# Feed-forward gate and up as pairs of seven half-depth products, hidden rows through DRAM, the down projection as its own stage

## The chip, the cores and the metric

One core of one Trainium2 chip runs the whole program. The metric is device time in microseconds (us) from launch to end, median of several runs. Five engines work side by side, each strictly in the order of its own program: PE (matrix products), DVE (vector), ACT (scalar and lookup functions), POOL (GpSimd) and SP, which here only issues DMAs. Waits between engines are semaphores.

## The reference, cut to what matters

Two blocks run one after the other on a sequence of 1024 tokens of width 1024, in fp32. The change concerns the feed-forward half of the first block:

```python
D_FF = -(-8 * D_MODEL // (3 * 256)) * 256          # 2816 = 22 chunks of 128
xn = rms_norm(x, ffn_norm_g[l])
gate, up = jnp.split(xn @ w_gate_up[l], 2, axis=-1)
x = x + (jax.nn.silu(gate) * up) @ w_down[l]
```

After it the second block (modulation, projections, window attention, convolution, a mixture of 16 experts) follows, and the change leaves its arithmetic as it was.

## The kernel before, in words

Every fp32 operand is held as a high and a low fp32r part, and a product is three matrix instructions: high by high, high by low, low by high (`mm3`, L64 to L67). Raw weights come by DMA into tiles `wst`; ACT copies the high part to `wh` (L58) and DVE subtracts to get `wl` (L59). That pair of instructions is `split`. `Weights.get` hands out the next converted piece and, before that, converts as many pieces ahead as `ahead` says; `fill` issues the next weight DMA on SP when a staging tile is free.

The feed-forward works on chunks of 128 of the 2816 hidden rows, 22 in all, in five parts of 5, 5, 4, 4, 4 chunks. `xn` holds the normed tokens, transposed, as eight tiles of 128 x 1024. For each chunk `columns` (L475) multiplies gate over the full depth of 1024 and two halves of 512 tokens, then up: 2 x 2 x 8 x 3 = 96 matrix instructions of 128x512. DVE scales gate by the token's 1/rms (`rsb`, L1100), ACT takes Silu (L1101), DVE multiplies by up (L1107) and by 1/rms (L1108), and the hidden rows are split to `hH` and `hL` at once. After each part its rows are multiplied with `w_down` in two groups of four output columns (`columns_k`, L279) and added to the resident `x1` (L1124). Between chunks `mods` (L1077) loads one of 48 pieces of the second block's modulation weights and accumulates it with two or four DVE instructions (L1056, L1058).

The second block already has a stage of the kind that the change adds: `quads` multiplies two weight columns as a 2 x 2 block matrix with seven half-depth products in place of eight. `seven` makes the weight combinations on POOL (L153, L154, L158, L162), `quarters` makes those of the tokens. The order on each engine is the order in which the Python code calls it; there is no scheduler.

Of the kernel before, what the change touches and what calls it, by code (L numbers as in the profile page):

```python
# [18 lines left out]
P = 128  # L19
# [3 lines left out]
def fused(tc, x, mix_norm_g, w_in, b_f, sgu_ln_g, sgu_ln_b, w_s, b_s, out_norm_g, w_out,  # L23
# [45 lines left out]
    class Weights:  # L69


        def __init__(self, es, units, side=R, stage=3, hl=3, ahead=2, scols=2112, pcols=1056, name="w"):
# [12 lines left out]
            self.wait, self.spare, self.halves, self.tmp = [], [], False, None  # L85
# [35 lines left out]
        def fill(self):  # L121
            while self.ndma < self.lim:
# [11 lines left out]
                if axis == "s":  # L134
                    self.wait.append(t)
                    if len(self.wait) == 2:
                        self.todo.extend(self.seven(*self.wait))
                        self.wait = []
                else:
                    for i in range(n):  # L140
                        s = t[:, i * cut:(i + 1) * cut, :] if axis == "k" else t[:, :, i * cut:(i + 1) * cut]
                        self.todo.append((lambda s=s, pre=pre: ([f(s) for f in pre], s)[1], int(i == n - 1)))
                self.ndma += 1

        def seven(self, a, b):
# [15 lines left out]
            def make4():  # L161
# [117 lines left out]
    def columns_k(W, n, rH, rL, ks, evac, cut=None, mid=()):  # L279
# [654 lines left out]
    npre = len(units) + 5 * len(pairs)  # L934
# [140 lines left out]
    xh = lambda k, hf: xn[k][0][:, hf * 512:(hf + 1) * 512]  # L1075
    xhl = lambda k, hf: xn[k][1][:, hf * 512:(hf + 1) * 512]
# [8 lines left out]
    def fw_done():  # L1085
        nonlocal psg, pmo
        es_fw.close()
        psg = pool(es_sg, "psg", 2)
        pmo = pool(es_mo, "pmo", 2)

    psg = pmo = None
    for f0, n in parts:
        hT = []
        for f in range(f0, f0 + n):
            sg = [None, None]

            def ev_gate(hf, ps):
                cs = slice(hf * 512, hf * 512 + 512)
                sg[hf] = psg.tile([P, 512], F32, name="sg")
                DVE.tensor_tensor(sg[hf], rsb[:, cs], ps, op=OP.mult)  # L1100
                act(sg[hf], sg[hf], AF.Silu)  # L1101

            hH, hL = phh.tile([P, T], F32R, name="hH"), phh.tile([P, T], F32R, name="hL")

            def ev_up(hf, ps):
                cs = slice(hf * 512, hf * 512 + 512)
                DVE.tensor_tensor(sg[hf], sg[hf], ps, op=OP.mult)  # L1107
                DVE.tensor_tensor(sg[hf], sg[hf], rsb[:, cs], op=OP.mult)  # L1108
                split(hH[:, cs], hL[:, cs], sg[hf])

            if f:
                columns(W, xh, xhl, KD, ev_gate)
                mods()
                columns(W, xh, xhl, KD, ev_up)
            else:
                columns_k(W, 2, xh, xhl, range(KD), lambda c, hf, ps: (ev_gate, ev_up)[c](hf, ps),
                          mid={(FM[0], 1): ffn_rs, (FM[1], 1): lambda: (spread(rsb, rs1), fw_done()), (FM[2], 1): lambda: W.prime(1)})
            hT.append((hH, hL))
            mods()
# [12 lines left out]
    es_s1.close()
# [72 lines left out]
    d_y = dram.tile([KD, P, T], F32, name="d_y")  # L1205
    d_gc = dram.tile([KD, P, T], F32, name="d_gc")
# [50 lines left out]
    rs1b = pool(es_x1, "prs1", 1, R).tile([P, T], F32, name="rs1b")  # L1257

# [22 lines left out]
    W.halves = True  # L1281
# [872 lines left out]
```

## Time and profile before

| | us |
|---|---|
| median of 3 runs | 2988.65 (2987.81 to 2989.24) |
| profiled execution, its own time | 2987.78 |
| its span, first to last instruction | 2985.8 |
| feed-forward of the first block, first to last product | 485.5 to about 1225 |
| seven-product stage of the second block | about 1378 to 1765 |
| PE busy over the span | 2859.5 (96%) |

The profile gives each engine's busy time. A matrix instruction of 128x512 is shown with 0.39 us, but one starts every 0.227 us since they are pipelined; a steady PE is read from the starts, not from the durations. DVE and ACT instructions overlap a little too: in a run without waits a DVE instruction of 128x512 starts 0.60 us after the one before it, although it is shown with 0.68 or 0.69 us.

### The profile page before, as it was taken

How to read it: one execution, taken by the hardware profiler on the slowest of the kernel's cores; microseconds unless marked ns; L12 is line 12 of the kernel's file. 1: busy time of each engine (PE TensorE's matmuls, PEld its weight loads, DVE VectorE, ACT ScalarE, POOL GpSimd, SP SyncE). 2: the span in 40 equal slices, each digit the busy share in tenths (PEclk: the TensorE clock that was granted, in tenths of full speed). 3: DMA queues.
4: the chain of work that ended last, by engine and by line, in shares of the span. 5: the costliest groups of instructions: out<-in, count | busy, mean ns of one | idle time of the engine just before them, and what ended most of it. 6: DMA issues, size and time to landing. Idle time of an engine off the chain costs nothing.

```text
span 2985.8 us, 37222 instructions
## 1 busy us (share of the span) xinstructions
PE 2859.5 (96%) x13943; PEld 2389.1 (80%) x13943; DVE 1911.1 (64%) x2741; ACT 1362.7 (46%) x2127; POOL 596.9 (20%) x607
## 2 busy tenths in 40 slices
PE   8999999999999999999999989899899789999997
PEld 7887878888888888887888877777788678888885
DVE  4446854645354444876666643888732579999998
ACT  5346943211111212522223331788622468888886
POOL 2301322000000000334444411233121302111113
PEclk9999999999999999999999999999999889999998
DMA  5120140322222221242222264000343689999998
GB/s 201 36 78 22 42 150 29 105 79 95 67 99 85 99 74 61 94 146 78 85 85 85 91 227 162 15 15 15 124 150 137 229 309 373 371 378 377 376 376 289
DMA packets 295236, 441.27 MB, mean 148 GB/s; under 512 B 14300, under 2 KB 143040, under 8 KB 294928
## 3 DMA queue, kind: packets, MB, share of 16 engines
q1 hardware_dynamic: 278048, 379.73, 36.8%
q0 software_dynamic: 15520, 58.11, 5.7%
q8 instruction: 109, 1.79, 0.2%
q10 hardware_dynamic: 1488, 1.06, 0.1%
q14 instruction: 71, 0.58, 0.1%
HBM read 380.62 MB, written 58.23 MB: 147 GB/s over the span
## 4 chain that ended last, share of the span: by engine, by line
PE 81%; DVE 7%; ACT 4%; issue 4%; DMA 3%; POOL 1%; SPq 0%; POOLq 0%; DVEq 0%; ACTq 0%
PE b L67 24%; PE b L65 24%; PE b L66 24%; PE pt L1614 1%; DVE pl L1632 1%; PE b L1995 1%; DVE sm L1595 1%; PE po L1644 1%; DVE wl L59 1%; DVE qs L1499 1%; PE pt L777 1%; DMA y<-d_y 1%; DMA d_x<-b,idxT 1%; PE po L1645 1%; PE b L1837 0%
## 5 line engine op out<-in xcount | busy, mean ns | idle before, releaser
L59 DVE TENSOR_TENSOR wl<-wst,wh 128x1024 fp32r<-128x1024 f32 (+3 forms) x620 | 714.3, 1181 | 256.6 <-ACT wh L58 248.9
L58 ACT ACTIVATE wh<-wst 128x1024 fp32r<-128x1024 f32 (+3 forms) x620 | 594.9, 976 | 458.1 <-PE b L66 190.8
L65 PE MATMUL b<-xn,wh 128*128 128x512 f32 x1040 | 408.1, 392 | 6.8 <-ACT xn L58 5.8
L67 PE MATMUL b<-xn,wl 128*128 128x512 f32 x1040 | 406.9, 391 | 3.7 <-DVE wl L59 3.7
L66 PE MATMUL b<-xn,wh 128*128 128x512 f32 x1040 | 406.8, 391 | 0.5 <-DVE xn L59 0.5
L65 PE MATMUL b<-wh,a 128*128 128x512 f32 x768 | 302.4, 394 | 0.2 <-ACT a L58 0.2
L66 PE MATMUL b<-wl,a 128*128 128x512 f32 x768 | 299.9, 391 | 0.8 <-DVE wl L59 0.8
L67 PE MATMUL b<-wh,a 128*128 128x512 f32 x768 | 299.8, 390 | 0.4 <-DVE a L59 0.4
L65 PEld LDWEIGHTS b<-xn,wh 128*128 128x128 f32 x1040 | 196.4, 189 | 47.9 <-ACT xn L58 6.2
L67 PEld LDWEIGHTS b<-xn,wl 128*128 128x128 f32 x1040 | 196.3, 189 | 46.4 <-DVE wl L59 5.2
L66 PEld LDWEIGHTS b<-xn,wh 128*128 128x128 f32 x1040 | 196.2, 189 | 41.7 <-DVE xn L59 1.0
L67 PEld LDWEIGHTS b<-wh,a 128*128 128x128 f32 x768 | 144.5, 188 | 31.1 <-DVE a L59 1.1
L66 PEld LDWEIGHTS b<-wl,a 128*128 128x128 f32 x768 | 144.7, 188 | 30.6 <-DVE wl L59 1.6
L65 PEld LDWEIGHTS b<-wh,a 128*128 128x128 f32 x768 | 144.8, 188 | 29.7 <-ACT a L58 0.7
L2037 POOL DMA_INDIRECT d_x<-b,idxT x15 | 65.8, 4388 | 470.9 <-DVE b L2031 470.9
L241 POOL TENSOR_SCALAR small<-small 128x1 f32<-128x1 f32 (+3 forms) x15 | 5.7, 383 | 768.7 <-ACT xn L1156 680.2
L65 PE MATMUL b<-hH,wh 128*128 128x512 f32 x352 | 137.7, 391 | 0.0
L67 PE MATMUL b<-hH,wl 128*128 128x512 f32 x352 | 137.1, 389 | 0.0
L66 PE MATMUL b<-hL,wh 128*128 128x512 f32 x352 | 136.9, 389 | 0.0
L58 ACT ACTIVATE hH<-sg 128x512 fp32r<-128x512 f32 x44 | 27.8, 632 | 202.7 <-DVE sg L1108 202.7
L1101 ACT ACTIVATE sg<-sg 128x512 f32<-128x512 f32 x44 | 27.7, 632 | 179.7 <-DVE sg L1100 179.7
L1595 DVE CUSTOM_DVE_ANT_0 sm<-sp,mk,nsk 128x640 f32<-128x640 f32 (+1 forms) x128 | 107.0, 837 | 1.2 <-PE sp L1584 1.0
(567 smaller groups left out, 6297.5 us busy)
## 6 DMA issues: line engine op xcount, KB each, us to landing
wst<-in_w_exp_gate_dram SPq DMA_DIRECT2D x128, 512.0 KB, 11.7
wst<-in_w_exp_up_dram SPq DMA_DIRECT2D x128, 512.0 KB, 10.7
wst<-in_w_exp_down_dram SPq DMA_DIRECT2D x128, 512.0 KB, 11.2
wst<-in_w_in_dram SPq DMA_DIRECT2D x74, 512.0 KB, 4.7
mw<-in_w_mod_dram SPq DMA_DIRECT2D x48, 512.0 KB
wst<-in_w_gate_up_dram SPq DMA_DIRECT2D x44, 512.0 KB, 4.0
wst<-in_w_down_dram SPq DMA_DIRECT2D x16, 512.0 KB, 3.8
wst<-in_w_out_dram SPq DMA_DIRECT2D x10, 512.0 KB, 4.7
```

The lines of the kernel that those rows point to most:

```text
L58: act(h, src, AF.Copy)
L59: DVE.tensor_tensor(l, src, rd(h), op=OP.subtract)
L65: PE.matmul(ps, lh, rh, start=start, stop=False)
L66: PE.matmul(ps, lh, rl, start=False, stop=False)
L67: PE.matmul(ps, ll, rh, start=False, stop=stop)
L777: PE.transpose(pt[:, b * P:(b + 1) * P], sm[:, (k0 + b) * P:(k0 + b + 1) * P], ident)
L1499: DVE.tensor_tensor(q[64:128, cs], pt[64 * o:64 * o + 64], rd(q[0:64, cs]), op=OP.subtract)
L1595: DVE.tensor_tensor_reduce(sms[n][:, :nk], sps.pop(n)[:, 256:256 + nk], (mk if i else mk0)[:, :nk], -0.125, nsk[:, hd:hd + 1], op0=OP.add, ...
L1614: PE.transpose(pt[:, hh * P:(hh + 1) * P], sms[4 * u + hh][:, kb * P:(kb + 1) * P], ident)
L1632: DVE.tensor_tensor(pl, pt, rd(ph), op=OP.subtract)
L1644: PE.matmul(pos[u], v, ph, start=kb == 0, stop=False)
L2037: nc.gpsimd.indirect_dma_start(out=d_x2, out_offset=bass.IndirectOffsetOnAxis(ap=idxT[:, e:e + 1], axis=0), in_=y, in_offset=None, compute ...
```

## The change

The first three chunks run gate and up as before. During chunks 1 and 2 `quarters_x` forms four combinations of the token quarters (`TX`). From chunk 3 on, gate and up of a chunk are one pair of weight columns and go through `quads` with seven products of four depth tiles, 84 matrix instructions. The scaling by 1/rms is now a POOL instruction (`times`), four of them for each pair, between the DVE sum and ACT's Silu. The products gate x up are formed at the start of the next pair (`hidden_out`), and the raw hidden rows go to DRAM by a DMA that POOL issues. `x1` goes to DRAM as well, for the time in which its place holds `TX`. After chunk 21 a stage of its own reads the hidden rows back, splits them (`h_in`), reads `x1` back and does the down projection, with four calls of `mods` after each group of columns. DRAM tiles `d_y` and `d_gc` of the second block become one tile for each index.

```diff
+    NCL = 3
+    for f in range(FF):
+        units += [(wsrc(w_gate_up, 0, KD, c * P, P), *(("s", 0) if f >= NCL else ("c", P))) for c in (f, FF + f)]
...
+    for k in range(KD):
+        nc.gpsimd.dma_start(d_xs[k], x1[k])
...
+    def quarters_x(k):
+        a11, a12, a21, a22 = [halft(n) for n in ("s", "u", "c1", "c2")]
+        for o, i, j in ((a11, 0, 0), (a12, 0, 1), (a22, 1, 1), (a21, 1, 0)):
+            DVE.tensor_tensor(o, *[rd(a[:, k, :]) for a in XQ[i, j]], op=OP.add)
+        for o, x, y in ((a11, a12, a11), (a12, a22, a12), (a22, a22, a11), (a21, a21, a22)):
+            DVE.tensor_tensor(o, x, y, op=OP.subtract)
+        for i, t in ((1, a11), (3, a12), (2, a22), (4, a21)):
+            h, l = TX[i]
+            split(h[:, k, :], l[:, k, :], t)
+
+    def hidden_out(h, c1, c2, su, f):
+        DVE.tensor_tensor(h[:, h1], su["u"], c2, op=OP.mult)
+        DVE.tensor_tensor(h[:, h0], su["s"], c1, op=OP.mult)
+        nc.gpsimd.dma_start(d_h[f], h)
...
+            if f == NCL - 1:
+                W.ahead = 4
...
+            while flush:
+                flush.popleft()()
+            c1, c2 = halft("c1"), halft("c2")
+            def times(x, cs):
+                POOL.tensor_tensor(x, x, rsb[:, cs], op=OP.mult)
+                return x
+            def gate(x, cs):
+                act(x, times(x, cs), AF.Silu)
+            su = {}
+            quads(W, SEVX, halft, lambda s, b: gate(plus(c1, s, b), h0),
+                  lambda u, b: (gate(plus(u, u, b), h1), su.update(u=u)),
+                  lambda s, b: (times(plus(s, s, b), h0), su.update(s=s)), lambda s, b: times(plus(c2, s, b), h1))
+            flush.append(lambda hr_=hr_, c1=c1, c2=c2, su=su, f=f: hidden_out(hr_, c1, c2, su, f))
+            mods()
...
+    for _ in range(2):
+        h_load(next(nxt))
...
+            for _ in range(4):
+                mods()
```

`quads` itself is moved up and takes the weights, the tokens and the tiles as arguments:

```python
after = [lambda: act(s, bk[0], AF.Copy), lambda: q11(s, bk[1]),
         lambda: DVE.tensor_tensor(s, s, bk[2], op=OP.add),
         lambda: DVE.tensor_tensor(u, s, bk[3], op=OP.add),
         lambda: (DVE.tensor_tensor(s, s, bk[4], op=OP.add), q22(s, bk[3])),
         lambda: q12(u, bk[5]), lambda: q21(s, bk[6])]
```

Products are numbered 1 to 7 below, and so are the seven weight halves of a pair. Half 3 and half 4 need L153 and L154 on POOL, half 5 needs L158, half 6 needs L162. With `ahead` at 4, the call of `get` for product i converts half i+4, so halves 1 to 4 of the next pair are converted during products 4 to 7 of this one.

First place, POOL in the feed-forward. Before, it has the sums of squares (`s1`), the two small instructions for 1/rms, and then nothing until two small ones for the context tokens (`small`, 128x2) and the last part's squares (`xn`):

```order
L1005 TENSOR_TENSOR s1_3918<-s1_3918,hH_4574 128x512
L1005 TENSOR_TENSOR s1_3918<-s1_3918,hH_4577 128x512
L241 TENSOR_SCALAR small_71<-small_71 128x8
L242 TENSOR_TENSOR small_71<-small_71,mhalf_66 128x8
L241 TENSOR_SCALAR small_71<-small_71 128x2
L242 TENSOR_TENSOR small_71<-small_71,mhalf_66 128x2
L1174 TENSOR_TENSOR xn_8900<-xn_8900,xn_8972 128x512 x2
```

Now each pair has nine, shown from the scaling of `c2` of one pair to that of `c1` of the next (`s1` holds 1/rms by then, `hr` the finished rows):

```order
L1182 TENSOR_TENSOR c2_5276<-c2_5276,s1_3907 128x512
L153 TENSOR_TENSOR ws1_5373<-wst_5164 128x512
L154 TENSOR_TENSOR ws2_5374<-ws1_5373,wst_5162 128x512
L1182 TENSOR_TENSOR u_5278<-u_5278,s1_3907 128x512
L1182 TENSOR_TENSOR s_5277<-s_5277,s1_3907 128x512
L1139 DMA d_h4_4598<-hr_5271 128x1024
L158 TENSOR_TENSOR wst_5164<-wst_5162,wst_5164 128x512
L162 TENSOR_TENSOR wst_5162<-wst_5162,ws2_5374 128x512
L1182 TENSOR_TENSOR c1_5424<-c1_5424,s1_3907 128x512
```

The combinations for halves 5 and 6 stand behind the DMA of the rows before, and those for halves 3 and 4 behind the scaling of `c2`.

Second place, DVE over the end of a chunk. Before (`sg` gate, then hidden rows; `acc0`, `acc1` the modulation sums):

```order
L59 TENSOR_TENSOR wl_5184<-wst_4893,wh_5183 128x1024
L1100 TENSOR_TENSOR sg_5214<-s1_3918,b_5189 128x512
L1100 TENSOR_TENSOR sg_5242<-s1_3918,b_5217 128x512
L1058 SCALAR_TENSOR_TENSOR acc0_5035<-mw_5245,s2_70,acc0_5035 128x512 x2
L1058 SCALAR_TENSOR_TENSOR acc1_5038<-mw_5245,s2_70,acc1_5038 128x512 x2
L59 TENSOR_TENSOR wl_5252<-wst_4961,wh_5251 128x1024
L1107 TENSOR_TENSOR sg_5214<-sg_5214,b_5257 128x512
L1108 TENSOR_TENSOR sg_5214<-sg_5214,s1_3918 128x512
L59 TENSOR_TENSOR hL_5182<-sg_5214,hH_5181 128x512
```

Now (`b` the PSUM banks of the products, `c1` the first tile of the next pair):

```order
L314 TENSOR_TENSOR s_5426<-s_5426,b_5508 128x512
L326 TENSOR_TENSOR c2_5425<-s_5426,b_5490 128x512
L59 TENSOR_TENSOR wl_5505<-ws2_5525,wh_5504 128x512
L326 TENSOR_TENSOR u_5427<-u_5427,b_5530 128x512
L59 TENSOR_TENSOR wl_5547<-ws1_5524,wh_5546 128x512
L326 TENSOR_TENSOR s_5426<-s_5426,b_5550 128x512
L1099 SCALAR_TENSOR_TENSOR acc0_5259<-mw_5565,s2_70,acc0_5259 128x512 x2
L1099 SCALAR_TENSOR_TENSOR acc1_5262<-mw_5565,s2_70,acc1_5262 128x512 x2
L1137 TENSOR_TENSOR hr_5420<-u_5427,c2_5425 128x512
L1138 TENSOR_TENSOR hr_5420<-s_5426,c1_5424 128x512
L59 TENSOR_TENSOR wl_5547<-wst_5321,wh_5546 128x512
L59 TENSOR_TENSOR wl_5598<-wst_5319,wh_5597 128x512
```

The sum of product 6 (`u`) stands behind the conversion of half 3, which needs POOL; the products of the finished rows (L1137, L1138) stand behind the modulation sums.

Third place, ACT. Before:

```order
L58 ACTIVATE wh_5183<-wst_4893 128x1024
L1101 ACTIVATE sg_5214<-sg_5214 128x512
L1101 ACTIVATE sg_5242<-sg_5242 128x512
L58 ACTIVATE wh_5251<-wst_4961 128x1024
L58 ACTIVATE hH_5181<-sg_5214 128x512
```

Now, from half 3 of a pair to half 1 of the next but one:

```order
L58 ACTIVATE wh_5377<-ws2_5374 128x512
L1186 ACTIVATE u_5278<-u_5278 128x512
L58 ACTIVATE wh_5377<-ws1_5373 128x512
L58 ACTIVATE wh_5429<-wst_5164 128x512
L310 ACTIVATE s_5426<-b_5433 128x512
L58 ACTIVATE wh_5429<-wst_5162 128x512
L1186 ACTIVATE c1_5424<-c1_5424 128x512
L58 ACTIVATE wh_5466<-wst_5164 128x512
L58 ACTIVATE wh_5466<-wst_5319 128x512
```

Each Silu (L1186) now waits for a POOL scaling and has a weight conversion right behind it.

## Rows read from the trace of the kernel before

**Rows 1.** The page: busy time of each engine, and the chain by engine.

```profile
PE 2859.5 (96%) x13943; PEld 2389.1 (80%) x13943; DVE 1911.1 (64%) x2741; ACT 1362.7 (46%) x2127; POOL 596.9 (20%) x607
...
PE 81%; DVE 7%; ACT 4%; issue 4%; DMA 3%; POOL 1%; SPq 0%; POOLq 0%; DVEq 0%; ACTq 0%
```

**Rows 2.** Stretches: length, each engine busy (instructions), PE clock, DMA share, GB/s.

```profile
780.00:1080.00 300.00, 300.00 (x1344) 248.94 (x1343) 131.38 (x179) 48.09 (x61) 0.00 (x0) 1.00 0.27 86
1478.00:1578.00 100.00, 100.00 (x443) 82.79 (x442) 63.05 (x86) 31.21 (x53) 47.77 (x37) 1.00 0.26 85
...
1785.00:1790.00 5.00, 2.67 (x6) 1.80 (x7) 1.23 (x1) 1.41 (x2) 0.00 (x0) 0.50 0.70 286
```

**Rows 3.** Timeline of PE: start, duration, line, operation; one seven-product piece of twelve.

```profile
1482.32 0.39 PE L65 MATMUL b<-T2h,wh 128*128 128x512 f32 x1
...
1485.04 0.39 PE L65 MATMUL b<-T1h,wh 128*128 128x512 f32 x1
```

**Rows 4.** Timeline of POOL at a pair's end in the second block's stage.

```profile
1534.73 0.58 POOL L1399 DMA_DIRECT2D d_y<-y  x1 [0.30 <-POOL y L1396]
...
1536.40 1.31 POOL L158 TENSOR_TENSOR wst<-wst 128x512 f32<-128x512 f32 x1
1537.65 1.30 POOL L162 TENSOR_TENSOR wst<-wst,ws 128x512 f32<-128x512 f32 x1
1538.90 1.30 POOL L153 TENSOR_TENSOR ws<-wst 128x512 f32<-128x512 f32 x1
1540.28 1.63 POOL L154 TENSOR_TENSOR ws<-ws,wst 128x512 f32<-128x512 f32 x1
```

**Rows 5.** Timeline of DVE in that stage: a run without waits, one beside POOL.

```profile
1394.45 0.68 DVE L1374 TENSOR_TENSOR c<-s,b 128x512 f32<-128x512 f32 x1
...
1398.05 0.67 DVE L1362 TENSOR_TENSOR s<-s,b 128x512 f32<-128x512 f32 x1
1398.76 0.69 DVE L1374 TENSOR_TENSOR c<-s,b 128x512 f32<-128x512 f32 x1
...
1538.41 2.36 DVE L59 TENSOR_TENSOR wl<-wst,wh 128x512 fp32r<-128x512 f32 x1 [3.50 <-ACT wh L58]
```

**Rows 6.** Timeline of ACT at the same place.

```profile
1537.74 0.63 ACT L58 ACTIVATE wh<-wst 128x512 fp32r<-128x512 f32 x1 [2.19 <-POOL wst L158]
...
1538.99 1.16 ACT L58 ACTIVATE wh<-wst 128x512 fp32r<-128x512 f32 x2
```

**Rows 7.** DVE by line and form, 1380 to 1700 us: busy, mean ns, idle before.

```profile
L59 DVE TENSOR_TENSOR wl<-wst,wh 128x512 fp32r<-128x512 f32 x85 | 85.6, 1023 | 29.2 <-ACT wh L58 29.2
L1374 DVE TENSOR_TENSOR c<-s,b 128x512 f32<-128x512 f32 x33 | 22.5, 681 | 0.6
```

**Rows 8.** The modulation tile's instructions: nanoseconds minimum, median, maximum.

```profile
L1058 DVE SCALAR_TENSOR_TENSOR acc<-mw,s,acc x112: 743/751/754, 519.7 to 1147.5; 128x512 f32<-128x512 f32 x112
L1056 DVE TENSOR_SCALAR acc<-mw,s x16: 475/477/484, 519.2 to 1115.3; 128x512 f32<-128x512 f32 x16
```

**Rows 9.** Timeline of POOL, then ACT, at the feed-forward's start.

```profile
494.24 6.11 POOL L1005 TENSOR_TENSOR s<-s,hH 128x512 f32<-128x512 f32 x4 [28.49 <-ACT hH L1003]
501.98 0.20 POOL L241 TENSOR_SCALAR small<-small 128x8 f32<-128x8 f32 x1 [1.63 <-DVE small L277]
502.26 1.65 POOL L242 TENSOR_TENSOR small<-small,mhalf 128x8 f32<-128x8 f32 x1
...
507.83 1.09 ACT L269 ACTIVATE s<-b 128x512 f32<-128x512 f32 x2 [12.16 <-PE b L268]
```

**Rows 10.** Tile y of the second block: a result through DRAM and its split.

```profile
L1407 SPq DMA_DIRECT2D y<-d_y x4: 338/338/339, 1717.8 to 1770.8; - x4
L58 ACT ACTIVATE xn<-y x4: 1042/1043/1056, 1750.9 to 1789.6; 128x1024 fp32r<-128x1024 f32 x4
L59 DVE TENSOR_TENSOR xn<-y,xn x4: 1218/1224/1225, 1752.0 to 1790.7; 128x1024 fp32r<-128x1024 f32 x4
...
DMA to landing us min/median/max: 2.9/2.9/3.3
```

**Rows 11.** Timeline of PE across its longest wait in that stretch.

```profile
1780.65 0.39 PE L67 MATMUL b<-xn,wl 128*128 128x512 f32 x1
1786.86 0.80 PE L65 MATMUL b<-xn,wh 128*128 128x512 f32 x1 [5.83 <-ACT xn L58]
...
1792.55 0.63 PE L67 MATMUL b<-xn,wl 128*128 128x512 f32 x1
1792.98 0.63 PE L65 MATMUL b<-xn,wh 128*128 128x512 f32 x1
...
1794.33 0.40 PE L66 MATMUL b<-xn,wh 128*128 128x512 f32 x1
```

More of the change, by code (lines that the diff above doesn't have):

```diff
@@ L83, in __init__ @@
             self.ready = deque()
[L85 removed]
+            self.wait, self.spare, self.tmp = [], [], None
             if hl:
@@ L1083, in fused @@
     FM = (4, 6, 7)
[L1085 to L1112, printed above, removed]
-                mods()
[L1114 to L1119, printed above, removed]
@@ new lines, in fused @@
+    while flush:
+        flush.popleft()()
+    W.spare.clear()
+    while modq and modq[0][1]:
+        mod_load(*modq.popleft())
+    while modr:
+        mod_sum(modr.popleft())
+    es_mo.close()
+    es_xq.close()
+    es_T.close()
+    es_s1.close()
+    es_x1 = ExitStack()
+    px1 = pool(es_x1, "px1", 1, R)
+    x1 = [px1.tile([P, T], F32, name=f"x1_{k}") for k in range(KD)]
+    rs1b = px1.tile([P, T], F32, name="rs1b")
+    phh = pool(es_f, "phh", 5, R)
+    pmo = pool(es_mo, "pmo2", 2)
@@ new lines, in fused, with h_load, h_split, h_in @@
+    hraw = deque()
+    def h_load(f):
+        hraw.append(phr.tile([P, T], F32, name="hr"))
+        nc.sync.dma_start(hraw[-1], d_h[f])
+    def h_split():
+        h, l = phh.tile([P, T], F32R, name="hH"), phh.tile([P, T], F32R, name="hL")
+        src = hraw.popleft()
+        split(h, l, src)
+        return h, l
+    nxt = iter(range(FF))
+    def h_in():
+        r = h_split()
+        for f in nxt:
+            h_load(f)
+            break
+        return r
+    for _ in range(2):
+        h_load(next(nxt))
@@ L1127, in fused, with step @@
-    while modr:
-        mod_sum(modr.popleft())
-    assert not modq
+            if not i and not c0:
+                for k in range(KD):
+                    nc.sync.dma_start(x1[k], d_xs[k])
+            hn, nn = [], parts[i + 1][1]
+            def step(p0):
+                while len(hn) < min(nn, p0 + 2 + 5 - n):
+                    hn.append(h_in())
+            columns_k(W, 4, hv(0), hv(1), range(n), lambda c, hf, ps: DVE.tensor_tensor(
+                x1[c0 + c][:, hf * 512:(hf + 1) * 512], x1[c0 + c][:, hf * 512:(hf + 1) * 512], ps, op=OP.add), 2,
+                mid={(p0, 3): (lambda p0=p0: step(p0)) for p0 in range(0, n, 2)} if c0 else ())
@@ L1130, in fused @@
+            if c0:
+                step(n)
+            for _ in range(4):
+                mods()
+        hTs = hn
+    while modq or modr:
+        mods()
     es_mo.close()
-    es_sg.close()
-    es_s1.close()
+    es_hr.close()
+    pxn = pool(es_w, "pxn", 2 * KD)
+    xt = lambda dt: pxn.tile([P, T], dt, name="xn")
     A1 = cols(8)
@@ L1204, in fused @@
     d_ga = dram.tile([KD, P, T], F32, name="d_ga")
-    d_y = dram.tile([KD, P, T], F32, name="d_y")
-    d_gc = dram.tile([KD, P, T], F32, name="d_gc")
+    d_y = [dram.tile([P, T], F32, name=f"d_y{j}") for j in range(KD)]
+    d_gc = [dram.tile([P, T], F32, name=f"d_gc{j}") for j in range(KD)]
     d_q = dram.tile([P, NT, 1024], F32, name="d_q")
```

142 lines of the change are left out of this document (92 added, 50 removed).

## The prediction

> **What bounds the kernel now.** I read the page first. PE is busy for 96% of the span and holds 81% of the chain that ended last [rows 1], so the next view is the table of stretches. In the feed-forward PE is busy for all of 300 us while DVE has work for 131, ACT for 48 and POOL for none; the second block's seven-product stage, the only one like the stage to come, also keeps PE at 100%, with POOL at 48 and DVE at 63 of 100 us [rows 2]. Its PE timeline gives the price: twelve instructions from 1482.32 to 1485.04 make 0.2267 us each [rows 3]. A chunk's gate and up cost 96 x 0.2267 = 21.76 us before, and 84 x 0.2267 = 19.04 us as a pair. Whether that is saved is decided off PE, so I read the timelines of POOL, DVE and ACT in the stage that exists, where the same instructions stand [rows 4 to 7], and follow them through the new order.
>
> **What goes.** For 19 chunks twelve instructions go: 228 x 0.2267 = 51.7 us of PE. If PE remained the bound, this would be the gain.
>
> **What the pairs cost: one lap.** Four POOL scalings, a POOL DMA and four POOL weight combinations are interleaved with DVE sums, ACT Silus and weight conversions so that they close a ring in which each step waits for the one before, and no step of it is PE. Prices per step, with the start of the next engine included: a DVE run of n is 0.60 n + 0.13 (eight starts from 1394.45 to 1398.76, of which the last, which uses the one before, comes 0.71 after it) [rows 5]; POOL 1.25 in a run and 1.34 to ACT's start, 1.38 where L154 uses L153 [rows 4, 6]; ACT 0.67 for one, 1.20 for two [rows 5, 6]; a POOL DMA 0.30 + 0.58 after its data [rows 4]. From half 7 of a pair on:
>
> 1. DVE: half 7, sum 3, next half 1, sum 4, next half 2, sum 5, c2: 4.44
> 2. POOL: scale c2, L153, L154: 3.97
> 3. ACT: high part of next half 3: 0.67
> 4. DVE: its low part, then sum 6 (u): 1.33
> 5. POOL: scale u: 1.34
> 6. ACT: Silu of u, high part of half 4: 1.20
> 7. DVE: its low part, then sum 7 (s): 1.33
> 8. POOL: scale s: 1.34
> 9. DVE: the second product of the finished rows, then the DMA issue on POOL: 1.57
> 10. POOL: L158, L162: 2.59
> 11. ACT: high part of half 6: 0.67
> 12. DVE: its low part, then c1 of the next pair: 1.33
> 13. POOL: scale c1: 1.34
> 14. ACT: Silu of c1, high part of half 7: 1.20
>
> Together 24.3 us, already above 21.76. Looking ahead by four halves does not help: step 14 holds half 7 behind a Silu on the same engine, and step 4 holds a finished product's sum behind a conversion.
>
> Between steps 7 and 9 DVE also has the modulation sums: four for each of the first pairs, two for the last ones. They are shown with 0.75 where a plain sum of 0.69 steps by 0.60 [rows 5, 8], so I step them by 0.66; with the first product of the rows (0.60) this is 3.25 or 1.9 us. They can lie beside step 8 (lap 26.2, or 24.9) or be added to it (27.6, or 26.2). The trace bounds both: a DVE instruction that reads two SBUF tiles took 2.36 instead of 0.69 while POOL ran without a gap, and L154 took 1.63 instead of 1.30 beside it [rows 4, 5]; 85 such conversions average 1.02 us, and sums that read a PSUM bank 0.68 [rows 7]. The two engines shut each other out there, so I take the sum.
>
> The Trainium skill (SBUF — State Buffer, Who interferes with whom) says the same and more sharply: a VectorE instruction with two SBUF inputs and a GpSimd instruction that reads SBUF hold a shared port in turn, one waits for the whole of the other, and a VectorE instruction with one SBUF input does not take part. By the rule the lap is 27.6; if the rows meant only a slower pace it would be nearer 26.2. The trace agrees with the rule (2.36 beside 0.69, and 0.68 for the sums from PSUM).
>
> Eighteen laps end in pairs 2 to 19: 15 x 27.6 + 3 x 26.2 = 492.6. The first pair needs its 19.0 us and about 3 of lag; about 4 go off, since the first lap starts with halves converted and in each fourth load two of the instructions take 0.48 [rows 8]. Together 511 us, against 19 x 21.76 = 413.4: **98 us more**. Bounds of this term: all of the modulation hidden, 18 x 24.3 + 18 = 455, so 42 more; every one of the eight POOL instructions at 1.63, so 2.6 more a lap, about 146 more.
>
> PE then waits in each lap, longest before product 5: about 6 us. After such a wait (1780.65 to 1786.86) the granted clock was 0.50, the lower level of 1.2 GHz, and instructions came every 0.43 us until about 1794 [rows 2, 11]. That makes products 5 and 6 some 3.3 us later. Product 5 is wanted in step 1 only after steps 11 to 14, so I cost this at nothing; the cover is less than 2 us.
>
> **Start of the feed-forward.** POOL has eight DMA issues for `x1`, 8 x 0.58 = 4.6 us [rows 4], between the sums of squares and 1/rms. Before, 1/rms was done at 503.9 and ACT took the spread from PE at 507.8 [rows 9], so nearly 4 us, less the transposes, cover it. I take 2; bounds 0 and 5. The token splits come in 16 halves instead of ten pieces and keep ahead of PE, which needs a depth tile only every 12 x 0.2267 = 2.7 us.
>
> **Chunks 1 and 2.** Each half of a chunk (48 x 0.2267 = 10.9 us) gets twelve DVE instructions more, 7.2 us, beside about 3 of its own. It fits, but the last twelve can start only after chunk 2's last sum and must give the combination for product 3 after 5.4 us. I take 2; bounds 0 and 8.
>
> **Into the down projection.** What was hidden before is now a stop. In the last pair sum 7 stands behind a Silu and two full conversions (1.04 and 1.22 each [rows 10]), then modulation, scaling and the two products: 7.3 us after PE's last product. The DMA issue and landing are 0.9 + 2.9, the read into the tile that this DMA leaves is 0.3 + 2.9, the split 1.04 + 1.22 [rows 10]: together 16.6, during which PE can run only three instructions. Then comes the lower clock, 16 instructions 0.2 us slower, about 3. I take 19; bounds 8 (one DMA instead of two in the way) and 30.
>
> **The down stage.** PE has the same 1056 instructions. DVE gets 22 splits of 1.22 and four modulation loads behind each group: per group of 120 instructions (27.2 us) about 5 of sums, 4 of conversions, 6 of splits and 5 of modulation, 20 together, which fits. Behind a late load on SP stand weights that are staged several pieces ahead. I take 2; bounds 0 and 15. The tiles `d_y` and `d_gc` have the same writes and reads as before; I take 0, at best PE's wait of 5.83 there goes [rows 11].
>
> **Sum**, against the profiled execution's 2987.8 (span 2985.8): 98 + 2 + 2 + 19 + 2 = 123 more, 3110.8. The median of the runs is 0.9 higher, so I say 3111.
>
> **Rivals.**
>
> *PE stays the bound.* For it: the existing stage of the same kind runs PE at 100% [rows 2]. There, POOL has one or two multiplications a pair and its Sigmoids wait for DVE alone, so the ring has no steps 2 (first part), 5, 8 and 13. Time: 2987.8 - 51.7 + 25 = 2961, faster. Chance 7%. The Trainium skill (Perfetto Trace Analysis, Identifying the Most-Contended Engine) would have the busiest engine relieved first, which is this case; no row here shows that POOL's new work keeps off the path.
>
> *The ring, but DVE and POOL beside each other.* 15 x 26.2 + 3 x 24.9 + 18 = 486, 72 more, in all 3085. For it: sums from PSUM are not slowed. Against it: the 2.36. Chance 14%.
>
> *The low clock for the whole stage.* If the waits keep PE at 0.43 an instruction, a pair takes 35.9 us: 19 x (35.9 - 21.76) = 269 more, 3281. For it: the row after 1786.86. Against it: slower products fill the waits that would cause it. Chance 3%.
>
> That no products are saved is excluded: the order of PE is shorter by 228 rows.
>
> **How the numbers follow.** The forecast as worked out has 76%. Its own bounds, 3032 to 3192, need all terms at one end together; 3060 to 3150 holds it nearly always and rival two, and leaves out rivals one and three (10%) and some 8% of the tails. A difference below 0.2% (6 us) can't be told from none. Faster 0.07, same 0.01, slower 0.92.
>
> **What would show it.** Right: in the stage of pairs one pair follows the next after 26 to 28 us, PE is busy for about seven tenths of it and waits before product 5 for DVE's low part `wl`; ACT waits for POOL before each Silu; POOL instructions of 128x512 number eight a pair; PE stands still for some 16 us before the first `hH` product. Wrong: pairs that follow each other after 19 us with PE at 100% (then my ring has a step that does not wait), or after 24 (then modulation is hidden), or PE instructions every 0.43 us throughout.

## The result, and the profile after

The changed kernel takes 3119.1 us (median of 4 runs, 3115.5 to 3121.0), the kernel before 2988.9 on the same chip: ratio 1.043, 95% interval 1.041 to 1.045. The profiled executions are 3115.5 and 2987.8 us, 127.7 apart. I followed the difference by place first. The sums of squares behind the feed-forward (L276 on tile `xn`) begin at 1230.4 us before and at 1358.8 after, 128.4 later; the second block adds nothing. Here is that group, before and then after (nanoseconds minimum, median, maximum, then first and last start):

```profile
L276 PE MATMUL b<-ones,xn x32: 164/250/271, 1230.4 to 1234.0; 128*128 128x1 f32 x32
...
L276 PE MATMUL b<-ones,xn x32: 164/250/352, 1358.8 to 1362.6; 128*128 128x1 f32 x32
```

The page of the changed kernel, busy time of each engine and the chain that ended last:

```profile
PE 2873.2 (92%) x13715; PEld 2378.2 (76%) x13715; DVE 2035.0 (65%) x2925; ACT 1415.2 (45%) x2241; POOL 813.1 (26%) x789
...
PE 68%; DVE 11%; issue 7%; POOL 6%; ACT 5%; DMA 2%; SPq 0%; POOLq 0%; ACTq 0%; DVEq 0%
```

PE has 228 instructions fewer than before and is busy for longer, and its share of the chain fell from 81% to 68% [rows 1]. The stretches tell where. Before, the whole feed-forward (start, length, busy time of PE, PEld, DVE, ACT, POOL, then PE's clock):

```profile
485.00:1226.00 741.00, 739.70 (x3341) 613.86 (x3342) 369.33 (x512) 153.97 (x213) 25.79 (x20) 1.00 0.26 83
```

and in the changed kernel the same work, then one lap of the pairs, from one store of hidden rows to the next:

```profile
485.00:1354.50 869.50, 753.09 (x3116) 602.64 (x3115) 494.35 (x696) 207.86 (x327) 242.57 (x202) 0.91 0.33 107
...
813.68:840.90 27.22, 21.34 (x84) 16.37 (x84) 14.28 (x20) 5.72 (x10) 11.20 (x10) 0.92 0.23 77
```

PE stood idle for 1.3 us before and for 116.4 after. In a lap it has its 84 instructions (19.04 us of work at full speed) and 27.22 us for them; no other engine is busy for more than 14.3 us of it. So nothing is full, and the time must lie in waits. Who waited for whom in the pairs, 550 to 1050 us (sum, times, longest):

```profile
DVE wl L59 <- ACT wh L58: 225.7, 71, 4.7
POOL c L1182 <- DVE c L326: 147.1, 36, 8.9
ACT wh L58 <- POOL wst L158: 144.2, 17, 10.9
ACT wh L58 <- POOL ws L154: 133.7, 18, 7.7
...
PE b L65 <- ACT wh L58: 81.3, 17, 5.9
POOL d_h L1139 <- DVE hr L1138: 60.5, 17, 6.1
...
DVE s L314 <- PE b L67: 0.2, 1, 0.2
```

DVE waits for ACT, ACT for POOL, POOL for DVE: three engines in a ring, with PE at its edge. PE waits for the ring, 81.3 us in all; DVE waited for a product of PE once, for 0.2 us. One lap of it on POOL's timeline (start, duration; in brackets the idle time ahead and who ended it), which answers to [rows 4]:

```profile
798.61 1.28 POOL L1182 TENSOR_TENSOR c<-c,s 128x512 f32<-128x512 f32 x1 [5.71 <-DVE c L326]
799.85 1.29 POOL L153 TENSOR_TENSOR ws<-wst 128x512 f32<-128x512 f32 x1
801.22 1.29 POOL L154 TENSOR_TENSOR ws<-ws,wst 128x512 f32<-128x512 f32 x1
804.57 1.29 POOL L1182 TENSOR_TENSOR u<-u,s 128x512 f32<-128x512 f32 x1 [2.07 <-DVE u L326]
808.45 1.73 POOL L1182 TENSOR_TENSOR s<-s,s 128x512 f32<-128x512 f32 x1 [2.59 <-DVE s L326]
813.68 0.58 POOL L1139 DMA_DIRECT2D d_h<-hr  x1 [3.50 <-DVE hr L1138]
814.28 1.27 POOL L158 TENSOR_TENSOR wst<-wst 128x512 f32<-128x512 f32 x1
815.50 1.28 POOL L162 TENSOR_TENSOR wst<-wst,ws 128x512 f32<-128x512 f32 x1
818.84 1.28 POOL L1182 TENSOR_TENSOR c<-c,s 128x512 f32<-128x512 f32 x1 [2.06 <-DVE c L326]
825.84 1.29 POOL L1182 TENSOR_TENSOR c<-c,s 128x512 f32<-128x512 f32 x1 [5.71 <-DVE c L326]
```

Between them stand DVE (for [rows 5])

```profile
803.20 0.69 DVE L59 TENSOR_TENSOR wl<-ws,wh 128x512 fp32r<-128x512 f32 x1 [4.67 <-ACT wh L58]
...
807.08 0.69 DVE L59 TENSOR_TENSOR wl<-ws,wh 128x512 fp32r<-128x512 f32 x1 [2.58 <-ACT wh L58]
807.69 0.68 DVE L326 TENSOR_TENSOR s<-s,b 128x512 f32<-128x512 f32 x1
808.28 3.89 DVE L1099 SCALAR_TENSOR_TENSOR acc<-mw,s,acc 128x512 f32<-128x512 f32 x4
...
821.34 0.69 DVE L59 TENSOR_TENSOR wl<-wst,wh 128x512 fp32r<-128x512 f32 x1 [2.58 <-ACT wh L58]
```

and ACT (for [rows 6]):

```profile
802.54 0.63 ACT L58 ACTIVATE wh<-ws 128x512 fp32r<-128x512 f32 x1 [7.42 <-POOL ws L154]
805.89 0.63 ACT L1186 ACTIVATE u<-u 128x512 f32<-128x512 f32 x1 [2.72 <-POOL u L1182]
...
816.81 0.63 ACT L58 ACTIVATE wh<-wst 128x512 fp32r<-128x512 f32 x1
820.16 0.63 ACT L1186 ACTIVATE c<-c 128x512 f32<-128x512 f32 x1 [2.72 <-POOL c L1182]
```

Go from start to start and you have the fourteen steps: POOL 798.61, ACT 802.54, DVE 803.20, POOL 804.57, ACT 805.89, DVE 807.08, POOL 808.45, and so on until POOL 825.84. The next section but one sets them beside the prediction.

PE's waits in the changed kernel, at the first pair, in two laps and at the hand-over to the down projection (for [rows 11]):

```profile
567.31 0.79 PE L65 MATMUL b<-t2h,wh 128*128 128x512 f32 x1 [4.21 <-ACT t2h L58]
569.18 0.80 PE L66 MATMUL b<-t2l,wh 128*128 128x512 f32 x1 [1.08 <-DVE t2l L59]
...
816.27 0.80 PE L65 MATMUL b<-t3h,wh 128*128 128x512 f32 x1 [4.71 <-ACT wh L58]
843.49 0.80 PE L65 MATMUL b<-t3h,wh 128*128 128x512 f32 x1 [5.88 <-ACT wh L58]
...
1077.05 1.87 PE L1108 MATMUL b<-ones,acc 128*128 128x1 f32 x8 [8.44 <-DVE acc L1099]
...
1086.02 0.80 PE L65 MATMUL b<-hH,wh 128*128 128x512 f32 x1 [4.49 <-ACT hH L58]
```

### The profile page after: what moved, and what is told of

It reads as the page before. It is cut to its first block, busy times and chain, and to the rows that moved or that the text cites. A ratio compares the mean times of both kernels' runs of the same rounds, so it can differ in the third digit from the quotient of the medians.

```text
span 3113.6 us, 37585 instructions
## 1 busy us (share of the span) xinstructions
PE 2873.2 (92%) x13715; PEld 2378.2 (76%) x13715; DVE 2035.0 (65%) x2925; ACT 1415.2 (45%) x2241; POOL 813.1 (26%) x789
## 4 chain that ended last, share of the span: by engine, by line
PE 68%; DVE 11%; issue 7%; POOL 6%; ACT 5%; DMA 2%; SPq 0%; POOLq 0%; ACTq 0%; DVEq 0%
PE b L67 19%; PE b L65 19%; PE b L66 19%; DVE acc L1099 1%; PE pt L1726 1%; DVE wl L59 1%; ACT wh L58 1%; PE b L2107 1%; POOL c L1182 1%; PE po L1756 1%; POOL wst L158 1%; POOL u L1182 1%; PE po L1757 1%; POOL ws L154 1%; POOL ws L153 1%
## 5 line engine op out<-in xcount | busy, mean ns | idle before, releaser
L59 DVE TENSOR_TENSOR wl<-wst,wh 128x1024 fp32r<-128x1024 f32 (+2 forms) x677 | 740.2, 1121 | 280.0 <-ACT wh L58 269.7
L58 ACT ACTIVATE wh<-wst 128x1024 fp32r<-128x1024 f32 (+2 forms) x677 | 610.3, 922 | 529.8 <-POOL wst L158 187.5
L59 DVE TENSOR_TENSOR wl<-ws,wh 128x512 fp32r<-128x512 f32 x78 | 53.6, 690 | 157.3 <-ACT wh L58 157.3
L65 PE MATMUL b<-xn,wh 128*128 128x512 f32 x368 | 145.6, 396 | 5.7 <-ACT xn L58 4.8
L67 PE MATMUL b<-xn,wl 128*128 128x512 f32 x368 | 145.1, 394 | 2.6 <-DVE wl L59 2.6
L66 PE MATMUL b<-xn,wh 128*128 128x512 f32 x368 | 145.1, 394 | 0.5 <-DVE xn L59 0.5
L58 ACT ACTIVATE wh<-ws 128x512 fp32r<-128x512 f32 x78 | 47.5, 622 | 177.5 <-POOL ws L154 134.4
L65 PE MATMUL b<-t3h,wh 128*128 128x512 f32 x76 | 46.5, 611 | 87.6 <-ACT wh L58 87.6
L1099 DVE SCALAR_TENSOR_TENSOR acc<-mw,s,acc 128x512 f32<-128x512 f32 x112 | 95.7, 864 | 29.3 <-DMA mw<-in_w_mod_dram 26.5
L1744 DVE TENSOR_TENSOR pl<-pt,ph 128x512 fp32r<-128x512 f32 x152 | 102.0, 686 | 7.9 <-ACT ph L1736 7.3
L1714 ACT ACTIVATE sm<-sm,tn 128x640 f32<-128x640 f32 (+1 forms) x128 | 103.0, 805 | 0.5 <-DVE tn L1707 0.3
```

The lines of the kernel that those rows point to most:

```text
L58: act(h, src, AF.Copy)
L59: DVE.tensor_tensor(l, src, rd(h), op=OP.subtract)
L65: PE.matmul(ps, lh, rh, start=start, stop=False)
L66: PE.matmul(ps, lh, rl, start=False, stop=False)
L67: PE.matmul(ps, ll, rh, start=False, stop=stop)
L1099: DVE.scalar_tensor_tensor(a, t[:, kk, :], sc, a, op0=OP.mult, op1=OP.add)
```

## The experiments

My theory: the pairs are paced by the ring of in-order queues, with DVE and POOL shutting each other out, and the rest is hand-over. Rivals: PE or its clock sets the pace; the same ring without the exclusion; the DRAM round trip and the separate stage cost the time. Twelve kernels were run, each against the kernel before on its chip. "Lap" is the distance between stores of hidden rows in the middle of the stage.

| run | median us | ratio to before, 95% | lap, us |
|---|---|---|---|
| changed kernel | 3119.1 | 1.041 to 1.045 | 27.2, 27.0 |
| e1_no_scale | 3008.0 | 1.005 to 1.009 | 20.95, 20.6 |
| e2_no_mods | 3133.6 | 1.047 to 1.051 | 24.7 |
| e3_order | 3095.9 | 1.034 to 1.038 | 26.1, 25.6 |
| e4_down_alone | 3020.1 | 1.009 to 1.013 | no pairs |
| e5_scale_dve | 3058.4 | 1.021 to 1.025 | 23.8, 23.4 |
| e6_up_in_down | 2997.5 | 1.002 to 1.004 | 20.0, 19.7 |
| e7_handover | 3111.8 | 1.039 to 1.043 | 27.2, 27.0 |
| e8_all | 2986.8 | 0.998 to 1.000 | 20.0, 19.7 |
| e9_first_store | 2985.3 | 0.997 to 0.999 | 20.0, 19.7 |
| e10_early_sums | 2984.6 | 0.997 to 0.999 | 20.0, 19.7 |
| e11_silu_later | 2975.9 | 0.994 to 0.997 | 19.04, 20.9 |
| e12_mods_mid | 3001.0 | 1.003 to 1.007 | 20.9 |

### The ring's links, one at a time

**Without the scalings.**

```diff
             def times(x, cs):
-                POOL.tensor_tensor(x, x, rsb[:, cs], op=OP.mult)
                 return x
```

> Leaves out the four multiplications by 1/rms in each pair (POOL's L1182), and nothing else; so POOL issues four weight combinations and one store per pair. Lap theory (the pair is paced by a chain that goes round through the in-order queues of DVE, POOL and ACT, with DVE and POOL keeping each other out): the chain loses four of its steps and falls below PE's own 19.04 us; 19.0 to 20.0 us from pair to pair, about 375 us for the 19 pairs where the changed kernel takes 513, whole run 2980 (2965 to 3000). Rival 1, queues without exclusion between DVE and POOL: 19.04 us, 362, run 2968. Rival 2, PE itself or its granted clock sets the pace: still 26 to 27 us, run 3115.

111 us less than the changed kernel: PE and its clock are out as the pace. But 139 were expected, and the lap stayed at 20.95 instead of 19 to 20. POOL's timeline in that run:

```profile
719.37 0.56 POOL L1139 DMA_DIRECT2D d_h<-hr  x1 [14.90 <-DVE hr L1138]
719.95 1.29 POOL L158 TENSOR_TENSOR wst<-wst 128x512 f32<-128x512 f32 x1
721.20 1.30 POOL L162 TENSOR_TENSOR wst<-wst,ws 128x512 f32<-128x512 f32 x1
```

and DVE's beside it:

```profile
714.89 2.98 DVE L1099 SCALAR_TENSOR_TENSOR acc<-mw,s,acc 128x512 f32<-128x512 f32 x4
...
721.94 4.02 DVE L59 TENSOR_TENSOR wl<-wst,wh 128x512 fp32r<-128x512 f32 x2 [2.87 <-ACT wh L58]
```

The four modulation sums take 2.98 us here, with POOL standing still, and 3.89 in the changed kernel, with a scaling on POOL beside them. POOL has nothing to do for 14.9 us, yet its weight combinations stand behind a store that waits for the hidden rows, which wait for the modulation sums. A smaller ring is left: last sum, modulation, rows, store, L158, ACT, DVE, and from there by DVE's sums and the two Silu to the next last sum. In it two DVE instructions of 0.69 take 4.02 while four POOL instructions run one after another.

**Without the modulation sums in the pairs.**

```diff
-            mods()
-            if f == NCL:
-                mods()
```

> No modulation sums in the pair stage; the same sums are all done in and behind the down stage. Lap theory with exclusion: every lap 24.3 to 24.8 us, all alike, 463 us for the 19 pairs (513 before this edit). Without exclusion: 24.3, 454. If PE's clock sets the pace: 26 to 27 still. The 20 moved loads and sums must be done later: 16 of them do not fit between the down products and come serially behind, 16 x 1.4 us = 22. Whole run by the lap theory 3119 - 50 + 22 = 3091 (3075 to 3105); if the sums were no part of the lap 3119 + 22 = 3141.

Two stores in a row on POOL of that run:

```profile
787.22 0.58 POOL L1139 DMA_DIRECT2D d_h<-hr  x1 [1.02 <-DVE hr L1138]
811.90 0.58 POOL L1139 DMA_DIRECT2D d_h<-hr  x1 [1.02 <-DVE hr L1138]
```

24.68 us apart, where the bare ring of the prediction was 24.3: the modulation adds 2.5 us to a lap that it takes part in, between the 1.9 of the ring without exclusion and the 3.25 of the plain sum. The total was missed: behind the pairs the moved work cost some 60 us and not 22, since PE waits 50.8 us there, five times, for the moved sums themselves (the waits' row `PE b L1108 <- DVE acc L1099`).

**The order alone.**

```diff
-        nc.gpsimd.dma_start(d_h[f], h)                # in hidden_out
...
-            while flush:
-                flush.popleft()()
...
+                  {1: lambda: flush and flush.popleft()()})    # mid of quads
-            flush.append(lambda hr_=hr_, c1=c1, c2=c2, su=su, f=f: hidden_out(hr_, c1, c2, su, f))
+            hidden_out(hr_, c1, c2, su, f)
+            flush.append(lambda hr_=hr_, f=f: nc.gpsimd.dma_start(d_h[f], hr_))
             mods()
```

> The same instructions in another order: the two products of the hidden rows stand on DVE ahead of the pair's modulation sums instead of behind them, and POOL's store of the hidden rows is issued after the second product of the next pair instead of ahead of its first. Lap theory with exclusion: the store no longer holds the weight combination of the next pair behind the modulation sums, but most of the chain stays, 26.0 to 26.5 us per pair, 495 us for the pairs, run 3101 (3090 to 3110). Without exclusion: 23.5 us, 443, run 3049. If order on the queues is not what paces the pair: 3119.

26.1 us a lap and 23 us in all, with the very same instructions. The ring without exclusion would have come to 23.5; this run counts most against it.

**The scalings on DVE.**

```diff
-                POOL.tensor_tensor(x, x, rsb[:, cs], op=OP.mult)
+                DVE.tensor_tensor(x, x, rsb[:, cs], op=OP.mult)
```

> The four scalings by 1/rms of each pair on DVE instead of POOL, all else as in the changed kernel: the same work, on the engine that is already busier. Lap theory with exclusion: four changes of engine leave the chain and a 1.28 us instruction becomes one of 0.69: 23.4 us per pair, 438 us for the 19 pairs, run 3044 (3030 to 3060). Without exclusion: 21.7 us, 406, run 3012. If DVE's amount of work were the bound, it would get longer: 27.2 + 4 x 0.69 = 30 us per pair, run over 3160.

More work on the busier of the two engines takes 61 us off the run, 14 fewer than expected. What remains is as in e1_no_scale: the store waits up to 17.8 us for DVE, and two low parts take 4.0 beside the POOL combinations freed by it.

### The down projection by itself

```diff
-    NCL = 3
+    NCL = FF = w_down.shape[0] // P        # all 22 chunks as plain columns
```

(the token sums and their tiles go, and the modulation sums are called once per chunk)

> No pairs: all 22 chunks as plain gate and up columns, as in the kernel before, but with the hidden rows through DRAM and the down projection as a stage of its own, and without the half-depth token sums. It shows what these cost by themselves. By the prediction's terms: 2988 + 2 (start) + 19 (hand-over) + 2 (down stage) = 3011 (3000 to 3030). Rival: the DRAM round trip and the separate stage are what costs, not the lap of the pairs: 3060 to 3110.

31 us and not 23. The round trip is a minor part: 3119.1 - 3020.1 = 99 us belong to the pairs and their token sums. PE in this kernel at the hand-over:

```profile
987.27 1.87 PE L1108 MATMUL b<-ones,acc 128*128 128x1 f32 x8 [10.36 <-DVE acc L1099]
990.28 0.80 PE L65 MATMUL b<-hH,wh 128*128 128x512 f32 x1 [1.15 <-ACT hH L58]
```

With a short one for `hL` 12.0 us are idle here, and 7.7 later, where a modulation product or the next columns wait for a PSUM bank (a piece of the memory that PE writes its results to) until DVE has added the last columns to `x1` (L1252); the same 3341 instructions of PE are besides busy for 751.7 instead of 739.7 us, at a mean clock of 0.98.

**The hand-over mended.**

```diff
+    phl = pool(es_hr, "phl", 4)                 # own tiles for the rows read back
...
-        hraw.append(phr.tile([P, T], F32, name="hr"))
-        nc.sync.dma_start(hraw[-1], d_h[f])
+        hraw.append(phl.tile([P, T], F32, name="hr"))
+        (nc.scalar if f < 4 else nc.sync).dma_start(hraw[-1], d_h[f])
...
-            mods()
-            if f == NCL:
+            if f < FF - 1:
+                mods()
+            if f < NCL + 2:
                 mods()
...
-    for _ in range(2):
+    for _ in range(4):
         h_load(next(nxt))
```

> The pairs as in the changed kernel; only the hand-over into the down projection is altered: four tiles of their own for the rows read back (two shared with the pairs before), the first four loads issued on ACT's queue instead of behind SP's weight fill, and no modulation sums in the last pair. The pairs' pace stays at 27.2 and 25.8. By the theory that the 18.7 us from the last pair's product to steady down products are the wait for the last pair's store and for SP's queue, they fall to about 8: run 3109 (3103 to 3114). If the wait were for the weights or the space, 3119.

The median is 7 lower and the profiled execution 12, as expected in size, though the 95% intervals of the two ratios overlap; PE's waits before `hH` are 3.47 and 1.65 there instead of 8.44, 0.76, 4.49 and 0.47. Why the four runs spread over 10 us (3103 to 3113) I did not find.

### Towards a version that gains

**The up half scaled in the down stage, the gate's on DVE, with the order above.**

```diff
-  (times(plus(s, s, b), h0), su.update(s=s)), lambda s, b: times(plus(c2, s, b), h1)
+  (plus(s, s, b), su.update(s=s)), lambda s, b: plus(c2, s, b)
...
         f, src = hraw.popleft()
+        if f >= NCL:
+            POOL.tensor_tensor(src, src, rsb, op=OP.mult)
```

> Three edits: the order of the run with the later store; the gate's two scalings on DVE; the up half's two scalings are taken out of the pairs and done once on the whole hidden row when it is read back for the down projection, on POOL, which has nothing to do there. Lap theory: the chain falls below PE's 19.04 us, 19.1 us per pair, 366 us for the pairs (513 in the changed kernel), run 3119 - 147 = 2972. The 19 instructions on POOL in the down stage (1024 wide, some 2.5 us each) may hold up DVE there: 0 to 15 more, so 2960 to 2995. If PE or its clock held the pairs at 21: run 3005.

20.0 us a lap: 122 us less than the changed kernel, 25 short of the expectation. 16 of these are the lap (0.9 for each of 18), 8 lie between the last store and L276 (289 us, 280 in the changed kernel); 6 of them are longer waits of PE for DVE's sums into `x1` (13.8 us, 7.7 in the changed kernel). Why these are longer is open: e8_all has the same scalings in that stage, and 8.6 us of such waits.

**Both**, the edits of e6_up_in_down and e7_handover in one kernel.

> The edits of the two runs before together. 2972 - 10 = 2962 (2945 to 2985), which is faster than the kernel before (2989) by 0.9%.

Level with the kernel before, though PE has 51.7 us less to do, and 25 us above the 2962 that was expected, as e6_up_in_down was above its own figure.

**The third chunk's store later**, in `flush` and no longer at the chunk's end:

```diff
-        if f < NCL:
+        if f < NCL - 1:
             nc.gpsimd.dma_start(d_h[f], hr_)
+        elif f < NCL:
+            flush.append(lambda hr_=hr_, f=f: nc.gpsimd.dma_start(d_h[f], hr_))
```

> The run with all edits, and one more: the store of the third chunk's hidden rows is not issued at the chunk's end but after the second product of the first pair. In the run before it stood on POOL's queue ahead of the first pair's weight combinations, held them for 20.5 us, and five of them then ran back to back while DVE formed the last token sums (one DVE instruction took 4.68 us there instead of 0.68); TensorE waited 7.6 us for the tokens of the third product. By the lap theory with exclusion the combinations now run ahead of those sums, the wait goes and the low clock behind it with it: 8 us less, 2979 (2970 to 2986). If the token sums themselves are late, whatever POOL does: 2987.

A miss: 6.6 us of the 7.6 stayed. The token sums begin at 560.46 behind the third chunk's last sums, and POOL's next combinations are freed at the same time anyway.

**The token sums a column earlier.**

```diff
             columns(W, xh, xhl, KD, ev_gate)
-            quarters_x(2 * f - 2)
+            quarters_x(0 if f == 1 else 3)      # step 2 ahead of the third chunk
...
-            quarters_x(2 * f - 1)
+            if f == 1:
+                quarters_x(1)
```

> The run before, with the token sums of the half-depth products one column earlier: the third and the fourth of their four steps stand on DVE behind the second chunk and behind the third chunk's gate column, instead of behind the third chunk's gate and up columns. If the wait of 6.6 us at the first pair's third product is for the last step's twelve instructions on DVE, which only begin when the third chunk is done, it goes, with the 1.1 us behind it and the low clock after it: 8 to 10 us less, 2976 (2970 to 2981), 0.45% faster than the kernel before. If the weight combinations on POOL are late by themselves: 2984.

The wait for the tokens went and one of 4.09 us for a weight conversion took its place; the first lap's store came 2 us sooner, and nothing of it is seen in the total, for which 2976 was expected.

**Silu behind the next conversion.**

```diff
-                act(x, times(x, cs), AF.Silu)
+                times(x, cs)
+                gated.append(lambda: act(x, x, AF.Silu))   # after the next product
```

> The run before, with each pair's two Silu on ACT behind the next weight conversion instead of ahead of it. In the run before, the pairs came every 20.0 us, 0.96 above TensorE's 19.04, and DVE stood without work only three times a pair, 1.2 us each, for a weight conversion on ACT; two of these conversions stood behind a Silu that waited for DVE's own scaling. If the chain through the two queues still sets the pace: 19.0 to 19.4 us per pair, 13 to 18 us less in all, 2968 (2962 to 2975), 0.7% faster than the kernel before. If the pace of 20.0 is set by DVE and POOL keeping each other out while the modulation sums run: 2984, unchanged.

Laps of 19.04 us, PE's own 84 x 0.2267, and 20.9 where eight modulation products are in between. The stretch of 300 us in this run, with PE busy throughout:

```profile
620.00:920.00 300.00, 300.00 (x1357) 249.48 (x1356) 265.01 (x341) 87.88 (x153) 96.58 (x76) 1.00 0.33 108
```

So the last 0.96 us of the lap was again a chain through two queues. DVE and POOL still hold each other up, with 1.62 us for a modulation sum here and 1.60 in the run before, but this no longer sets the pace. This is the fastest version: 0.5% (0.3 to 0.6) under the kernel before, and 8 us short of what was expected.

**The modulation where POOL rests.**

```diff
+                   3: lambda f=f: f < FF - 1 and mods(),       # mid of quads, fourth product
...
-            if f < FF - 1:
-                mods()
```

> The run with the later Silu, and the modulation sums of a pair placed on DVE behind its fourth product's sum, where POOL has nothing to do, instead of behind its last, where POOL forms weight combinations. If DVE and POOL keep each other out, a modulation sum (1.56 us on the mean in the run with the early token sums, 0.69 in the kernel before) falls back to 0.7, and 3.4 us of DVE's time per pair are freed; the pace is then at TensorE's 19.04 to 19.4, run 2966 (2958 to 2978). Rival: the sums now hold up the sums and splits that TensorE needs for its next products, 20 to 21 us per pair, run 2990 or more.

DVE by form in this run, 620 to 920 us (count, busy, mean ns, idle ahead):

```profile
L59 DVE TENSOR_TENSOR wl<-wst,wh 128x512 fp32r<-128x512 f32 x73 | 76.6, 1050 | 9.0 <-ACT wh L58 9.0
L1099 DVE SCALAR_TENSOR_TENSOR acc<-mw,s,acc 128x512 f32<-128x512 f32 x47 | 34.5, 751 | 42.4 <-DMA mw<-in_w_mod_dram 41.5
```

and in e11_silu_later, which differs from it only in where the modulation stands:

```profile
L1099 DVE SCALAR_TENSOR_TENSOR acc<-mw,s,acc 128x512 f32<-128x512 f32 x49 | 78.6, 1619 | 1.0
L59 DVE TENSOR_TENSOR wl<-wst,wh 128x512 fp32r<-128x512 f32 x75 | 55.6, 757 | 0.3
```

The exclusion is confirmed: with POOL at rest a modulation sum falls from 1.62 to 0.75 us, its time in the kernel before [rows 8] (the expectation has 0.69 there). The rival was right on the time: at that place its weights have not arrived (41.5 us of waiting for the DMA), and the low parts of the weights now meet POOL instead (1.05 for 0.76).

## Why the prediction was right, and where a term was off

Predicted 3111, measured 3119.1; 123 more for the profiled execution, measured 127.7. The mechanism was the one named. That the total came so close is partly luck: the pairs came out 6 us cheaper than forecast, the wait ahead of the first pair 6 dearer and the down stage 7 dearer, so that a good part of the errors cancelled.

**The lap.** Step by step, from the timelines of the lap that begins at 798.61:

| step | predicted | measured |
|---|---|---|
| 1 DVE run of seven | 4.44 | 4.50 |
| 2, 3 POOL three, ACT | 3.97, 0.67 | 3.93, 0.66 |
| 4, 5, 6 DVE, POOL, ACT | 1.33, 1.34, 1.20 | 1.37, 1.32, 1.19 |
| 7 DVE | 1.33 | 1.37 |
| 8, modulation and first product, 9 | 1.34 + 3.25 + 1.57 | 5.83 |
| 10 POOL two | 2.59 | 2.53 |
| 11, 12 ACT, DVE | 2.00 | 2.03 |
| 13, 14 POOL, ACT | 1.34, 1.20 | 1.32, 1.18 |
| lap | 27.6 | 27.23 |

Only step 8 with the modulation is off by more than 0.1: scaling and modulation share the time less strictly than a plain sum of both (POOL 1.73 for 1.29, four DVE instructions 3.89). The laps with two instructions were 25.8 (predicted 26.2), every fourth of the others 27.0. The 18 laps took 482.1 us, from the store at 596.40 to that at 1078.50, against 492.6, 10 less, of which 3 are the last lap (24.39). The prediction had taken 4 off for such laps, so the term of 98 for the pairs was 6 or 7 too large: from the first pair's first product (555.45) to the end of the last pair's last (1068.45) are 513 us, 8 of them the wait told under *Chunks 1 and 2* below, against 511. The e1, e2, e3 and e5 runs came within 1.0 us of what was expected of the lap with exclusion, and the ring without it was 0.4 to 2.6 below each of them; in e2_no_mods, with 0.4, the two can hardly be told apart. One sign was off: the wait before product 5 is for ACT's high part `wh`, and not for DVE's low part.

The Trainium skill (PSUM — Partial Sum Buffer, Engine vs sequencer instructions) calls the queues of ScalarE, VectorE and GpSimd strictly first in, first out. The trace agrees: in e1_no_scale POOL stood for 14.9 us at a store with four combinations behind it, which then ran one after another.

**The small terms.** *Start*: PE's first product came 0.6 us later (2 predicted). *Chunks 1 and 2*: 2 predicted; PE waited 4.21 and 1.08 us for the token combination, and went at a clock of 0.56 for 7.2 us behind it, 8 in all, the upper bound. The step counted twelve free instructions on DVE; in the trace the second of them took 3.46 us instead of 0.69 while two POOL combinations ran, released by the third chunk's store. *Down stage*: 2 predicted; PE's modulation products (L1108) have 7.7 us of waiting for DVE's sums into `x1` (L1257), where the kernel before has none (its L1067), and with the lower clock behind each wait it is about 9, which is also what the other terms leave of the 128.4. I had added up DVE's work per group and found that it fits; when it is done was not asked.

**Into the down projection**: 19 predicted; 14.2 us of waits (8.44, 0.76, 4.49, 0.47) and the slower products behind them make about 19: the stretch from 1068.45 to 1093.01 is 24.6 us long, and its products need 5.0 at full speed. The shape was different: not one stop of 16 us but two, because one of the two tiles was free while the last pair ran, so that the first row came early. The first stop ended with a modulation sum whose weights, on SP behind weight fills of 10.6 us, came 3.8 us late; the first row landed at about the same time (ACT began on it at 1076.80).

**PE's low clock** cost nothing in the laps, as said: after waits of 4.7 to 5.9 us PE began with one instruction every 0.43 us (granted clock 0.50 from 816.27 to 819.30), yet DVE waited for a product of PE only once in those 500 us. The saving of 51.7 us was real too: e11_silu_later shows PE at 19.04 a pair. Of the 52 us, 12 remain there; the rest is paid where e4_down_alone and e6_up_in_down show it, at the hand-over and in the down stage, and at the first pairs, whose laps are 20.1 and more.

## What to carry over

Before work is moved onto an idle engine, draw what every queue holds in order and go once around: an engine at 26% can set the pace when each of its instructions waits for one engine and is waited for by the next. Take the cheapest cut first: one or two instructions moved on their own queue (the rows and their store, a Silu) were worth 23 us in one case and 9 in another, with no work saved. And an operation that commutes with the next product (a scale per token) belongs in the stage whose engines have time.

## What the hardware showed that I had not expected

The exclusion between DVE and POOL is not turn by turn. DVE and POOL in e8_all, while the last token sums and the freed weight combinations meet; DVE:

```profile
558.98 0.68 DVE L1129 TENSOR_TENSOR s<-x00h,x00l 128x512 f32<-128x512 f32 x1
559.58 4.68 DVE L1129 TENSOR_TENSOR u<-x01h,x01l 128x512 f32<-128x512 f32 x1
564.19 1.75 DVE L1129 TENSOR_TENSOR c<-x11h,x11l 128x512 f32<-128x512 f32 x1
```

POOL:

```profile
559.95 1.30 POOL L158 TENSOR_TENSOR wst<-wst 128x512 f32<-128x512 f32 x1
561.19 1.29 POOL L162 TENSOR_TENSOR wst<-wst,ws 128x512 f32<-128x512 f32 x1
562.44 1.27 POOL L153 TENSOR_TENSOR ws<-wst 128x512 f32<-128x512 f32 x1
563.78 1.60 POOL L154 TENSOR_TENSOR ws<-ws,wst 128x512 f32<-128x512 f32 x1
```

One DVE instruction waited out three POOL instructions that followed each other without a gap, and ended 0.5 us after the fourth, L154, had begun; L154 reads L153's result and had a gap of 0.07 ahead of it, the first in that row. From there on both engines' instructions took 1.6 to 1.75 us, as if they took turns. The Trainium skill (SBUF — State Buffer, Who interferes with whom) has one engine hold the port for an instruction and the other blocked for it; the trace agrees, and shows a wait of three in a row.
